# Moving four small stages of a hybrid layer's dense part, and three weight loads past a loop

## The chip, the cores and the metric

The kernel runs on one core of a Trainium2 chip. The metric is device time in microseconds (us), of the whole program. TensorE (PE in the rows) does the matrix products; VectorE (DVE), ScalarE (ACT) and GpSimd (POOL) do the elementwise work; SyncE (SP) issues the weight transfers.

## The reference

One layer for 256 tokens of width 1024, in float32, and a last norm:

```python
u = rmsnorm(h, norm1_w)
rx, rg, qkv, z, a_in, b_in, ga, gb = split_columns(u @ w_in, IN_WIDTHS)
rx = causal_dwconv(rx, rnn_conv_w) + rnn_conv_b
h_rnn = rglru(rx, wa, ba, wx, bx, lam)            # tanh/exp/sqrt, then a scan over the tokens
y_a = (jax.nn.gelu(rg) * h_rnn) @ w_branch_a
q, k, v = jnp.split(jax.nn.silu(causal_dwconv(qkv, dn_conv_w)), 3, axis=-1)
q = l2norm(q); k = l2norm(k)                      # 8 heads of 128
g = -exp(dn_a_log) * softplus(a_in + dn_dt_bias); beta = sigmoid(b_in)
o = gated_delta_rule(q, k, v, g, beta)            # chunks of 64, a triangular inverse for each
y_b = (rmsnorm(o, dn_norm_w) * silu(z)) @ w_branch_b
h = h + (sigmoid(ga) * y_a + sigmoid(gb) * y_b) @ w_out
h = h + memory_cross_attention(rmsnorm(h, norm2_w), rmsnorm(mem, mem_norm_w), w_cq, w_ckv, w_co)
h = h + hierarchical_moe(rmsnorm(h, norm3_w), ...)   # 64 experts, 2 for each token
return rmsnorm(h, norm_f_w)
```

## The kernel before

**The dense part** lasts from 0 to 536 us. Its unit of work is one piece of a weight matrix. `load_w` has SP load 1 MB into one of two buffers `raw`; for each half ACT casts it (L169) to a high part, and the remainder is formed at L170, by DVE for the first half and by GpSimd for the second. Both parts stand in `whl`, whose four buffers hold two units. Then TensorE does 48 matmuls of 128x128 by 128x256 (L178, L179, L180: high by high, high by low, low by high). Units follow one another in the order of the code: 4 for the memory's keys (`wkv`), 5 x units (the recurrence's input), 5 g units (its gelu gate), 4 value units (the memory's values), z unit 0, 12 k, q and v units (`qkv_unit`, units 0 to 3 are k), then `wa` on the recurrence's output, the z and gate units that are left, and the later projections.

Between the units stand smaller stages that other engines share:
- `memory_norm` squares the memory (ACT, L212), adds up over columns (DVE, L214), sums over partitions by small matmuls (L349, L220), takes an inverse root in DVE steps (L121 to L125) and scales the keys on GpSimd (L353).
- `recurrence(h)`, once for each half of the blocks: ten matmuls (L385), tanh and exp on ACT, long DVE operations over 128x1280, a scan (L403), a product (L404), and the split for `wa` (L154 on ACT, L155 on DVE).
- `decay` makes the decay factors of the delta rule from small products (L292 to L303); `smalls` makes constants of the recurrence.
- `squares` transposes the 16 pieces of k by matmuls against the identity (L496) and squares them on ACT with a sum (L500).
- The inverses of the delta rule's triangles are a long chain on DVE (to L610) and then products on TensorE (L630 on). `meanwhile(n)` writes n of the eleven `fill` units (z units 1 to 3, gate units 0 to 7) ahead of those products; the others are used in the chunk loop and behind it, up to the split of the delta rule's output (L762, L155), which the next dense unit (`w_branch_b`) reads.

A scheduler sets the order of instructions on each engine, from the order of the code, with priority for what a unit's `load_w` does and for the conversion behind a q, k or v unit.

**The expert part** streams 192 weight matrices of 2 MB through a ring of 10 buffers (4 `ra`, 6 `rb`; L1101, L1106 and L1109 in `load_next`). Ahead of it stands `overflow()`, a loop on the chip (L1235, L1236) whose body runs only when an expert has too many tokens. The six `rb` buffers lie where the dense part had its data. A load that has to wait for its buffer holds up what is behind it in SP's queue.

Of the kernel before, what the change touches and what calls it, by code (L numbers as in the profile page):

```python
# [41 lines left out]
def hybrid_kernel(ctx: ExitStack, tc: tile.TileContext, A, out, dbg=None, until=99):  # L42
# [204 lines left out]
    for h in range(2):  # L247
        q = slice(4 * h, 4 * h + 4)
# [33 lines left out]
    def decay():  # L282

        softplus(ga[:, 1], ga[:, 0], ga[:, 2], ga[:, 3], ga[:, 4])
        SC.activation(ga[:, 5], bcast(P("alog"), 2), AF.Exp)
        V.scalar_tensor_tensor(ga[:, 0], ga[:, 1], -1.0, ga[:, 5], op0=OP.mult, op1=OP.mult)
        gm = small("gm", [2, 2, 8])
        for cc in range(2):
            V.tensor_scalar_mul(gm[:, :, cc], ga[:, 0], C("half", cc, 1))
        pg = bank("sm")  # L290
        g16, X0, X1 = [t.rearrange("p t h -> p (t h)") for t in (ga[:, 0], X[:, 0], X[:, 1])]
        T.matmul(pg[:, 0:16], C("tri"), g16, start=True, stop=True)  # L292
        T.matmul(pg[:, 16:32], C("same"), g16, start=True, stop=True)
        T.matmul(pg[:, 32:64], ones, gm.rearrange("p t c h -> p (t c h)"), start=True, stop=True)
        V.tensor_copy(X0, pg[:, 0:16])
        V.tensor_sub(X1, pg[:, 16:32], X0)
        SC.activation(EGL.rearrange("p t c h -> p (t c h)"), pg[:, 32:64], AF.Exp)
        pm = bank("sm")
        pmv = pm[:, :48].rearrange("p (q t a c) -> p q t a c", q=3, t=2, a=4)
        for par in range(2):  # L300
            for tt in range(2):
                for cc in range(2):
                    T.matmul(pmv[HALF[par], :, tt, :, cc], ident[:, cc * 64:cc * 64 + 64], X[:, :, tt, par::2],  # L303
                             start=True, stop=True)
        V.tensor_copy(TM[:, :3], pm[:, :48].rearrange("p (q n) -> p q n", q=3))
        SC.activation(TM[:, 3:5], TM[:, 0:2], AF.Exp)
        V.tensor_scalar_mul(TM[:, 5], TM[:, 3], -0.25)
# [28 lines left out]
    def smalls():  # L336

        V.tensor_scalar_mul(ch[:, 0], P("lam"), -1.0)
        softplus(ch[:, 1], ch[:, 0], ch[:, 2], ch[:, 3], ch[:, 4])
        V.tensor_scalar_mul(ch[:, 0], ch[:, 1], -4.0)  # L340
        V.tensor_scalar_mul(ch[:, 1], ch[:, 1], 2.0)
        V.tensor_scalar_mul(hb[:, 0], P("ba"), 0.5)
        V.tensor_scalar_mul(hb[:, 1], P("bx"), 0.5)
# [12 lines left out]
    def x_unit(un_):  # L356
        w = load_w(A["win"][un_])
        p = bank()
        for m in range(2):
            dense(p[:, m * 256:m * 256 + 256], w, m, u1)  # L360
        for m in range(2):
            r = un_ * 2 + m
            conv(xc[r // HB][:, r % HB], p[:, m * 256:m * 256 + 256], P("rcw", 4 * r, 4), P("rcb", r))

    def g_unit(un_):
        w = load_w(A["win"][5 + un_])
        p = bank()
        for m in range(2):
            dense(p[:, m * 256:m * 256 + 256], w, m, u1)
        sq = t2k("gsq")  # L370
        SC.activation(sq, p, AF.Square, scale=math.sqrt(0.044715))
        V.scalar_tensor_tensor(sq, sq, 1.0, p, op0=OP.add, op1=OP.mult)
        SC.activation(sq, sq, AF.Tanh, scale=math.sqrt(2.0 / math.pi))
        for m in range(2):
            r = un_ * 2 + m
            V.scalar_tensor_tensor(gg[r // HB][:, r % HB], two(sq)[:, m], 1.0, two(p)[:, m],
                                   op0=OP.add, op1=OP.mult)

    def recurrence(h):
        tr, ti = five("tr"), five("ti")  # L380
        for b in range(HB):
            r = h * HB + b
            p = bank("gd")
            for s in range(2):
                T.matmul(p[:, s * 256:s * 256 + 256], wg[h][:, s, b], xc[h][:, b], start=True, stop=True)  # L385
                SC.activation((tr, ti)[s][:, b], p[:, s * 256:s * 256 + 256], AF.Tanh,
                              bias=hb[:, s, r:r + 1], scale=0.5)

        a = five("lra")
        for b in range(HB):  # L390
            r = h * HB + b
            SC.activation(a[:, b], tr[:, b], AF.Exp, bias=ch[:, 0, r:r + 1], scale=ch[:, 0, r:r + 1])
            SC.activation(tr[:, b], tr[:, b], AF.Tanh, bias=ch[:, 1, r:r + 1], scale=ch[:, 1, r:r + 1])
        V.scalar_tensor_tensor(tr, a, 1.0, tr, op0=OP.add, op1=OP.mult)
        V.tensor_scalar(a, tr, -1.0, 1.0, op0=OP.mult, op1=OP.add)
        V.scalar_tensor_tensor(tr, tr, -2.0, tr, op0=OP.add, op1=OP.mult)

        SC.activation(tr, tr, AF.Sqrt, scale=-1.0 / 16)
        V.scalar_tensor_tensor(ti, ti, 1.0, xc[h], op0=OP.add, op1=OP.mult)
        V.tensor_mul(ti, ti, tr)  # L400
        V.memset(a[:, :, 0:1], 0.0)
        flat = lambda t: t.rearrange("p b t -> p (b t)")
        V.tensor_tensor_scan(flat(tr), flat(a), flat(ti), 0.0, OP.mult, OP.add)  # L403
        V.tensor_mul(ti, tr, gg[h])  # L404
        dump(f"gh{h}", ti)
        hi, lo = five("ghh", FR), five("ghl", FR)
        split(hi, lo, ti)
        gh.append((hi, lo))
# [16 lines left out]

    for un_ in range(5):
        x_unit(un_)
        if un_ == 0:
            memory_norm()
    smalls()  # L430
    for un_ in range(5):
        g_unit(un_)
    for h in range(2):
        recurrence(h)
    decay()
    for un_ in range(4):
        value_unit(un_)
    if until <= 1:
# [4 lines left out]
    def z_unit(un_):  # L443
        w = load_w(A["win"][22 + un_])
        p = bank()
        for m in range(2):
            dense(p[:, m * 256:m * 256 + 256], w, m, u1)
        th = t2k("zth")
        SC.activation(th, p, AF.Tanh, scale=0.5)
        for m in range(2):  # L450
            V.scalar_tensor_tensor(zf[:, un_, :, m], two(th)[:, m].rearrange("p (c t) -> p c t", c=4), 1.0,
                                   two(p)[:, m].rearrange("p (c t) -> p c t", c=4), op0=OP.add, op1=OP.mult)
# [21 lines left out]
    def qkv_unit(un_):  # L474
        w = load_w(A["win"][10 + un_])
        p = bank()
        for m in range(2):
            dense(p[:, m * 256:m * 256 + 256], w, m, u1)
        with tc.high_priority():
            tmp, th = two(t2k("cvt")), two(t2k("cth"))  # L480
            for m in range(2):
                conv(tmp[:, m], p[:, m * 256:m * 256 + 256], P("qcw", (un_ * 2 + m) * 4, 4))
            SC.activation(th, tmp, AF.Tanh, scale=0.5)
            dst = (kf, qf, vf)[un_ // 4]
            for m in range(2):
                V.scalar_tensor_tensor(dst[:, un_ % 4, :, m], th[:, m].rearrange("p (c t) -> p c t", c=4), 1.0,
                                       tmp[:, m].rearrange("p (c t) -> p c t", c=4), op0=OP.add, op1=OP.mult)


    NK = small("nk", [8, 16])  # L490

    def squares(f, dst):
        for q in range(4):
            p = bank("gd")
            for i, (tt, hp, c) in enumerate(units[q * 4:q * 4 + 4]):
                T.transpose(p[:, i * 128:i * 128 + 128], f[:, hp, c].rearrange("p b t -> p (b t)"), ident)  # L496
            sq = t2k("sqk", tag="tg")
            for i in range(4):
                o = slice(i * 128, i * 128 + 128)
                SC.activation(sq[:, o], p[:, o], AF.Square, accum_out=dst[:, q * 4 + i:q * 4 + i + 1])  # L500

    def key_sums():
        squares(kf, NK[:, 0])

        V.tensor_scalar(NK[:, 0], NK[:, 0], 0.25, EPS, op0=OP.mult, op1=OP.add)
        rsqrt(NK[:, 2], NK[:, 0], NK[:, 3])
        V.tensor_mul(NK[:, 3], NK[:, 2], NK[:, 2])
        V.scalar_tensor_tensor(NK[:, 5], TM[:, 2], 0.5, NK[:, 3], op0=OP.mult, op1=OP.mult)
        V.tensor_scalar_mul(NK[:, 6], NK[:, 5], 0.25)
        V.scalar_tensor_tensor(NK[:, 4], NK[:, 0], 0.5, NK[:, 2], op0=OP.mult, op1=OP.mult)  # L510
# [13 lines left out]
    for un_ in range(12):  # L524
        if un_ == 1:
            z_unit(0)
        qkv_unit(un_)
        if un_ == 7:
            key_sums()
        if un_ == 9:  # L530
            query_sums()
# [85 lines left out]
            un_ = next(fill)  # L617
            z_unit(4 + un_) if un_ < 0 else gate_unit(un_)

    meanwhile(4)  # L620


    flat8 = lambda t: t.rearrange("p n i -> p (n i)")
# [552 lines left out]
                T.matmul(into[tt][h], ct[:n, tt * 128:tt * 128 + 128], Y[:n, h * 512:h * 512 + 512],  # L1176
                         start=False, stop=False, skip_group_check=True)

    for k in range(NA + NB + 1):
        if k == NA:  # L1180
            nc.sync.dma_start(half, by_halves[:, :2048])
        load_next()
# [89 lines left out]
            combine(lambda tt: opw[:, tt], Y, SLOTS)  # L1272

    overflow()
    for e in range(NE - 3):
        expert(e)

# [159 lines left out]
```

## Time and profile before

| what | us |
|---|---|
| time, median of 3 runs | 1497.77 |
| lowest, highest run | 1497.13, 1500.68 |
| profiled execution, own time | 1499.66 |
| profiled execution, span | 1497.9 |
| TensorE busy | 1109.8 |
| VectorE busy | 539.3 |
| ScalarE busy | 349.4 |
| GpSimd busy | 199.9 |

Busy times are of the profiled execution, and every start time below counts from the start of its span. Its own time is 1.8 us more than the span, for what lies around it.

### The profile page before, as it was taken

How to read it: one execution, taken by the hardware profiler on the slowest of the kernel's cores; microseconds unless marked ns; L12 is line 12 of the kernel's file. 1: busy time of each engine (PE TensorE's matmuls, PEld its weight loads, DVE VectorE, ACT ScalarE, POOL GpSimd, SP SyncE). 2: the span in 40 equal slices, each digit the busy share in tenths (PEclk: the TensorE clock that was granted, in tenths of full speed). 3: DMA queues.
4: the chain of work that ended last, by engine and by line, in shares of the span. 5: the costliest groups of instructions: out<-in, count | busy, mean ns of one | idle time of the engine just before them, and what ended most of it. 6: DMA issues, size and time to landing. Idle time of an engine off the chain costs nothing.

```text
span 1497.9 us, 33194 instructions
## 1 busy us (share of the span) xinstructions
PE 1109.8 (74%) x14941; PEld 929.0 (62%) x14941; DVE 539.3 (36%) x1217; ACT 349.4 (23%) x741; POOL 199.9 (13%) x107
## 2 busy tenths in 40 slices
PE   6998999979999957876565675756656756666575
PEld 6997999979889945654444553545544545445453
DVE  7966786675757332221111211111202111111122
ACT  5356664417435510100000000000000000000011
POOL 2443332621136200000000000000000000000000
PEclk9999998989999978998898887887979889789897
DMA  7343352521268367999999999999999999999994
GB/s 254 138 170 130 123 170 92 191 85 58 84 243 325 116 273 327 426 425 425 426 426 427 425 427 424 425 426 427 425 426 425 426 426 427 425 425 427 426 424 177
DMA packets 42002, 477.40 MB, mean 319 GB/s; under 512 B 4481, under 2 KB 7169, under 8 KB 9857
## 3 DMA queue, kind: packets, MB, share of 16 engines
q1 hardware_dynamic: 40560, 472.56, 76.9%
q8 instruction: 119, 1.95, 0.5%
q10 hardware_dynamic: 1296, 2.68, 0.5%
q14 instruction: 27, 0.21, 0.0%
HBM read 474.17 MB, written 1.05 MB: 317 GB/s over the span
## 4 chain that ended last, share of the span: by engine, by line
DMA 56%; PE 5%; DVE 0%; issue 0%; ACT 0%; DVEq 0%; SPq 0%; ACTq 0%
DMA rb<-wed 13%; DMA rb<-weu 11%; DMA rb<-weg 11%; DMA ra<-weu 8%; DMA ra<-weg 8%; DMA ra<-wed 5%; PE gd L1140 2%; PE gd L1160 1%; PE mm L1176 1%; PE gd L1131 1%; PE mm L1208 0%; ACT fsq L1329 0%; DVE goh L1002 0%; PE gd L1313 0%; PE mm L1322 0%
## 5 line engine op out<-in xcount | busy, mean ns | idle before, releaser
L1140 PE MATMUL gd<-rb,xy 128*32 128x128 f32 x4864 | 182.0, 314 | 112.7 <-DMA rb<-weu 56.8
L1140 PEld LDWEIGHTS gd<-rb,xy 128*32 128x32 f32 x4864 | 160.1, 127 | 140.1 <-DMA rb<-weu 65.0
L170 POOL TENSOR_TENSOR whl<-raw,whl 128x1024 fp32r<-128x1024 f32 (+1 forms) x66 | 161.5, 2448 | 328.5 <-ACT whl L169 324.9
L1149 DVE SCALAR_TENSOR_TENSOR hid<-hid,gd 128x128 f32<-128x128 f32 x64 | 18.4, 288 | 440.7 <-ACT hid L1148 440.7
L1140 PE MATMUL gd<-ra,xy 128*32 128x128 f32 x3168 | 120.3, 317 | 72.4 <-DMA ra<-weg 35.2
L180 PE MATMUL mm<-u1h,whl 128*128 128x256 f32 x544 | 159.0, 292 | 6.9 <-DVE whl L170 6.4
L1140 PEld LDWEIGHTS gd<-ra,xy 128*32 128x32 f32 x3168 | 106.3, 128 | 88.6 <-DMA ra<-weu 40.1
L179 PE MATMUL mm<-u1l,whl 128*128 128x256 f32 x544 | 159.9, 294 | 0.0
L178 PE MATMUL mm<-u1h,whl 128*128 128x256 f32 x544 | 159.4, 293 | 0.0
L169 ACT CAST whl<-raw 128x1024 fp32r<-128x1024 f32 (+1 forms) x132 | 131.1, 1007 | 118.5 <-PE mm L180 87.9
L1148 ACT ACTIVATE hid<-gd 128x128 f32<-128x128 f32 x64 | 17.7, 277 | 532.0 <-PE gd L1140 532.0
L1160 PE MATMUL gd<-rb,hid 128*32 128x256 f32 x1216 | 94.5, 463 | 62.9 <-DMA rb<-wed 44.2
L1165 DVE COPY xy<-gd 32x256 f32<-32x256 f32 x126 | 52.6, 418 | 236.0 <-PE gd L1160 209.4
L1165 ACT COPY xy<-gd 32x256 f32<-32x256 f32 x126 | 45.8, 364 | 314.8 <-DVE xy L1165 314.8
L180 PEld LDWEIGHTS mm<-u1h,whl 128*128 128x128 f32 x544 | 107.9, 198 | 8.3 <-DVE whl L170 7.0
L179 PEld LDWEIGHTS mm<-u1l,whl 128*128 128x128 f32 x544 | 108.1, 199 | 2.1 <-issue 1.7
L1160 PEld LDWEIGHTS gd<-rb,hid 128*32 128x32 f32 x1216 | 47.5, 128 | 99.1 <-issue 65.1
L178 PEld LDWEIGHTS mm<-u1h,whl 128*128 128x128 f32 x544 | 108.0, 198 | 1.1 <-issue 0.7
L1009 POOL TENSOR_TENSOR gpw<-goh,ew 128x512 f32<-128x512 f32 x8 | 8.4, 1046 | 747.2 <-PE sm L1171 680.3
L170 DVE TENSOR_TENSOR whl<-raw,whl 128x1024 fp32r<-128x1024 f32 (+1 forms) x66 | 82.2, 1246 | 55.3 <-ACT whl L169 54.9
L1160 PE MATMUL gd<-ra,hid 128*32 128x256 f32 x800 | 62.1, 462 | 38.7 <-DMA ra<-wed 19.6
L1131 PEld LDWEIGHTS gd<-goh,hm 128*128 128x128 f32 x512 | 61.5, 194 | 15.8 <-issue 15.8
(420 smaller groups left out, 1782.2 us busy)
## 6 DMA issues: line engine op xcount, KB each, us to landing
rb<-weu SPq DMA_DIRECT2D x38, 2048.0 KB, 39.8
rb<-wed SPq DMA_DIRECT2D x38, 2048.0 KB, 39.8
rb<-weg SPq DMA_DIRECT2D x38, 2048.0 KB, 39.8
ra<-weg SPq DMA_DIRECT2D x26, 2048.0 KB, 39.9
ra<-weu SPq DMA_DIRECT2D x25, 2048.0 KB, 39.8
ra<-wed SPq DMA_DIRECT2D x25, 2048.0 KB, 39.8
raw<-win SPq DMA_DIRECT2D x34, 1024.0 KB, 4.9
raw<-wkv SPq DMA_DIRECT2D x7, 1024.0 KB, 4.9
```

The lines of the kernel that those rows point to most:

```text
L169: (hi[j].copy if hi[j] is SC else hi[j].tensor_copy)(w[:, 0], r)
L170: lo[j].tensor_sub(w[:, 1], r, w[:, 0].bitcast(FT))
L178: T.matmul(p, w(0, i, ms), u(0, i), start=(i == 0), stop=False)
L179: T.matmul(p, w(0, i, ms), u(1, i), start=False, stop=False)
L180: T.matmul(p, w(1, i, ms), u(0, i), start=False, stop=(i == k - 1))
L1131: T.matmul(o, hm[:, tt, c * 128:c * 128 + 128], g[:, tt], start=(tt == 0), stop=(tt == 1))
L1140: m = T.matmul(p[32 * j:32 * j + 32, o:o + 128], x[:, c], w(c)[:, j * 128:j * 128 + 128], start=(c == 0), stop=(c == 7), tile_position=(0, ...
L1148: SC.activation(tg, p[:, :128], AF.Tanh, scale=0.5)
L1149: V.scalar_tensor_tensor(th, tg, 1.0, p[:, :128], op0=OP.add, op1=OP.mult)
L1160: T.matmul(p[32 * q:32 * q + 32, :256], ht[:, 32 * j:32 * j + 32], w(j)[:, o:o + 256], start=(j == 0), stop=(j == 3), tile_position=(0, 32 ...
L1165: (SC.copy if q % 2 else V.tensor_copy)(Y[r:r + 32, q * 256:q * 256 + 256], p[32 * q:32 * q + 32, :256])
L1176: T.matmul(into[tt][h], ct[:n, tt * 128:tt * 128 + 128], Y[:n, h * 512:h * 512 + 512], start=False, stop=False, skip_group_check=True)
```

## The change

The order of the code changes in five places. `memory_norm` goes from behind x unit 0 to behind g unit 0, and `smalls` from ahead of the g units to behind g unit 2. `recurrence(1)` goes from ahead of the value units to ahead of qkv unit 2, and `decay` from there to ahead of qkv unit 4. `squares` of the keys is done in two parts: its first half behind qkv unit 6, its second in `key_sums`, where all of it stood. `meanwhile` writes six units ahead of the inverse's products and not four. Of the loads ahead of `overflow()` three are written behind it.

```diff
     for un_ in range(5):
         x_unit(un_)
+    for un_ in range(5):
+        g_unit(un_)
         if un_ == 0:
             memory_norm()
-    smalls()
-    for un_ in range(5):
-        g_unit(un_)
-    for h in range(2):
-        recurrence(h)
-    decay()
+        if un_ == 2:
+            smalls()
+    recurrence(0)
     for un_ in range(4):
         value_unit(un_)
...
-    def squares(f, dst):
-        for q in range(4):
+    def squares(f, dst, qs):
+        for q in qs:
...
     def key_sums():
-        squares(kf, NK[:, 0])
+        squares(kf, NK[:, 0], (2, 3))
...
     for un_ in range(12):
         if un_ == 1:
             z_unit(0)
+        if un_ == 2:
+            recurrence(1)
+        if un_ == 4:
+            decay()
         qkv_unit(un_)
+        if un_ == 6:
+            squares(kf, NK[:, 0], (0, 1))
         if un_ == 7:
             key_sums()
...
-    meanwhile(4)
+    meanwhile(6)
...
-    for k in range(NA + NB + 1):
+
+    HELD = 3
+    for k in range(NA + NB + 1 - HELD):
         if k == NA:
             nc.sync.dma_start(half, by_halves[:, :2048])
         load_next()
...
     overflow()
+    for _ in range(HELD):
+        load_next()
     for e in range(NE - 3):
         expert(e)
```

What the scheduler makes of it is shown at three places. The first is VectorE's order around the memory's norm. Before, its sum (L214) stands between steps of the first norm's inverse root (`ny`, L123 to L125), ahead of the products with the input (L244):

```order
L125 SCALAR_TENSOR_TENSOR ny<-ny 128x256
L214 TENSOR_REDUCE nx<-memsq 128x256
L123 TENSOR_TENSOR ny<-ny 128x256
L170 TENSOR_TENSOR whl<-raw,whl 128x1024
L124 SCALAR_TENSOR_TENSOR ny<-ny,nx 128x256
L125 SCALAR_TENSOR_TENSOR ny<-ny 128x256
L244 SCALAR_TENSOR_TENSOR xn<-xx,vecs,ny 128x256 x7
```

In the changed kernel it stands in the g units, behind a gelu unit's last operations (L376), and the first step on what TensorE made of it (L350, L222) follows one L170 later:

```order
L372 SCALAR_TENSOR_TENSOR gsq<-gsq,mm 128x512
L376 SCALAR_TENSOR_TENSOR gg<-gsq,mm 128x256 x2
L214 TENSOR_REDUCE nx<-memsq 128x256
L170 TENSOR_TENSOR whl<-raw,whl 128x1024
L350 TENSOR_SCALAR rsm<-sm 128x2
L222 TENSOR_SCALAR nx<-gd 128x256
L121 TENSOR_SCALAR rsm<-rsm 128x2
L372 SCALAR_TENSOR_TENSOR gsq<-gsq,mm 128x512
```

The sum moved behind all convolutions of the x units. On TensorE the small matmuls on it (L349, L220) stood at the start of the x units; they now stand behind the 14th matmul of g unit 2, the 350th that reads `u1`.

The second place is ScalarE's order where the first half of the recurrence ends (its split L154) and the second half's tanh (L386) began. Before:

```order
L423 ACTIVATE vm<-mm,rsm 128x256 x2
L169 CAST whl<-raw 128x1024 x2
L154 CAST ghh<-ti 128x1280
L423 ACTIVATE vm<-mm,rsm 128x256
L386 ACT_TABLE_LOAD
L386 ACTIVATE tr<-gd,hbias 128x256 x2
L169 CAST whl<-raw 128x1024
L386 ACTIVATE ti<-gd,hbias 128x256 x2
```

After, two casts of weights have passed the split, and the rows behind it go on with value and k units:

```order
L169 CAST whl<-raw 128x1024 x2
L423 ACTIVATE vm<-mm,rsm 128x256 x2
L154 CAST ghh<-ti 128x1280
L169 CAST whl<-raw 128x1024 x2
L423 ACTIVATE vm<-mm,rsm 128x256 x2
L169 CAST whl<-raw 128x1024
L312 ACTIVATE cvt<-mm,vecs 128x256
```

The tanh of the second half moved behind the first k unit and z unit 0. On VectorE the second half's scan stands, before and after, ahead of the last k units' conversions (L316, and the product that was L486 and is L485). In the changed kernel:

```order
L403 SCALAR_TENSOR_TENSOR tr<-lra,ti 128x1280
L316 SCALAR_TENSOR_TENSOR cvt<-mm,vecs,cvt 128x254
L404 TENSOR_TENSOR ti<-tr,gg 128x1280
L170 TENSOR_TENSOR whl<-raw,whl 128x1024
L316 SCALAR_TENSOR_TENSOR cvt<-mm,vecs,cvt 128x253
L305 COPY tm<-sm 128x48
L155 TENSOR_TENSOR ghl<-ti,ghh 128x1280
L316 SCALAR_TENSOR_TENSOR cvt<-mm,vecs,cvt 128x255
L485 SCALAR_TENSOR_TENSOR kf<-cth,cvt 128x4x64
```

TensorE's first eight transposes of the keys (L496, now L495) stand behind q unit 6, 48 dense matmuls ahead of the other eight; before, twelve stood together behind q unit 7, and four a little later.

The third place is VectorE's order behind the chain of the inverses, whose end is L610 (now L615). Before, one gate unit's product (L467) stands ahead of the operations on TensorE's first products (L639):

```order
L608 STREAM_TRANSPOSE sta<-sta 128x512
L170 TENSOR_TENSOR whl<-raw,whl 128x1024
L610 TENSOR_SCALAR stt<-sta,early_consts 128x16x32 x2
L467 SCALAR_TENSOR_TENSOR ya<-ath,ya 128x512
L634 STREAM_TRANSPOSE stt<-stt 128x512 x2
L639 TENSOR_TENSOR yb<-gd,early_consts 64x8x64 x4
```

After, two more L170 and one more gate product stand there:

```order
L613 STREAM_TRANSPOSE sta<-sta 128x512
L170 TENSOR_TENSOR whl<-raw,whl 128x1024
L615 TENSOR_SCALAR stt<-sta,early_consts 128x16x32 x2
L466 SCALAR_TENSOR_TENSOR ya<-ath,ya 128x512
L639 STREAM_TRANSPOSE stt<-stt 128x512 x2
L170 TENSOR_TENSOR whl<-raw,whl 128x1024
L466 SCALAR_TENSOR_TENSOR ya<-ath,ya 128x512
L170 TENSOR_TENSOR whl<-raw,whl 128x1024
L644 TENSOR_TENSOR yb<-gd,early_consts 64x8x64
```

On TensorE 220 dense matmuls, before 140, stand between the last matmul of the triangles and the inverse's first product; in exchange 72, before 171, are left between the last matmul of the chunk loop (L714) and the first of `w_branch_b`. SP's queue holds six `rb` loads ahead of the loop before, and four after; two stand behind it now. (The third held load waited for an `ra` buffer and stood behind the loop in both.)

## Rows read from the trace of the kernel before

**Rows 1.** The page's second part: GB/s in 40 equal slices of the span.
```profile
GB/s 254 138 170 130 123 170 92 191 85 58 84 243 325 116 273 327 426 425 425 426 426 427 425 427 424 425 426 427 425 426 425 426 426 427 425 425 427 426 424 177
```
**Rows 2.** The chain that ended last, one piece: start, length, what.
```profile
633.40 37.90 DMA rb<-weu
```
**Rows 3.** Waits of TensorE, 0 to 540 us: total us, times, longest.
```profile
PE mm L180 <- DVE whl L170: 8.3, 5, 3.9
PE gd L630 <- DVE stt L610: 7.6, 1, 7.6
PE gd L385 <- ACT tr L386: 6.5, 1, 6.5
PE gd L496 <- ACT sqk L500: 2.5, 1, 2.5
```
**Rows 4.** Busy us by stretch: PE, PEld, DVE, ACT, POOL; granted clock, DMA share, GB/s.
```profile
77.00:82.00 5.00, 5.00 (x26) 5.00 (x25) 4.19 (x9) 2.91 (x4) 1.25 (x1) 0.50 0.58 210
158.00:182.00 24.00, 24.00 (x202) 24.00 (x202) 22.32 (x20) 17.02 (x25) 10.77 (x5) 1.00 0.44 150
187.00:196.00 9.00, 8.75 (x60) 8.54 (x59) 7.96 (x14) 6.92 (x9) 2.23 (x1) 0.81 0.34 118
323.00:330.00 7.00, 7.00 (x34) 7.00 (x34) 2.94 (x6) 0.00 (x0) 0.00 (x0) 0.50 0.28 115
564.00:576.00 12.00, 5.56 (x132) 5.13 (x132) 0.30 (x1) 0.28 (x1) 0.00 (x0) 0.60 0.38 139
```
**Rows 5.** Timeline, memory's norm and g units: start, length, instruction, [idle before <- releaser].
```profile
24.68 2.00 ACT L212 ACTIVATE memsq<-memx 128x1024 f32<-128x1024 f32 x2
30.31 3.93 DVE L214 TENSOR_REDUCE nx<-memsq 128x256 f32<-128x2048 f32 x1
68.21 4.81 DVE L289 TENSOR_SCALAR gm<-ga,early_consts 128x16 f32<-128x16 f32 x2
68.37 4.62 POOL L353 TENSOR_TENSOR kt<-kt,ny 128x2048 f32<-128x2048 f32 x1 [2.82 <-DVE ny L125]
76.43 0.58 PE L180 MATMUL mm<-u1h,whl 128*128 128x256 f32 x1 [3.88 <-DVE whl L170]
92.80 0.63 ACT L373 ACTIVATE gsq<-gsq 128x512 f32<-128x512 f32 x1 [0.75 <-DVE gsq L372]
```
**Rows 6.** Timeline from the recurrence's first half to the last k product.
```profile
145.46 1.26 ACT L154 CAST ghh<-ti 128x1280 fp32r<-128x1280 f32 x1 [6.38 <-DVE ti L404]
148.39 0.84 ACT L386 ACTIVATE tr<-gd,hbias 128x256 f32<-128x256 f32 x2
186.81 0.39 PE L180 MATMUL mm<-u1h,whl 128*128 128x256 f32 x1 [1.94 <-DVE whl L170]
189.59 0.41 DVE L486 SCALAR_TENSOR_TENSOR kf<-cth,cvt 128x256 f32<-128x256 f32 x1
205.82 0.97 DVE L486 SCALAR_TENSOR_TENSOR kf<-cth,cvt 128x256 f32<-128x256 f32 x2 [0.76 <-ACT cth L483]
```
**Rows 7.** Timeline at the inverses.
```profile
319.57 1.18 DVE L170 TENSOR_TENSOR whl<-raw,whl 128x1024 fp32r<-128x1024 f32 x1
322.02 1.30 PE L630 MATMUL gd<-stt,ab 128*128 128x64 f32 x5 [7.58 <-DVE stt L610]
```
**Rows 8.** Timeline behind the chunk loop: its last matmuls, the output's last split.
```profile
393.97 0.87 PE L714 MATMUL gd<-sm,qf 128*64 128x128 f32 x10
410.97 0.69 DVE L155 TENSOR_TENSOR ol<-ynat,oh 128x512 fp32r<-128x512 f32 x1 [0.69 <-ACT oh L154]
```
**Rows 9.** Timelines of SP and PE, and the `rb` loads' landing, 535 to 580 us.
```profile
539.41 0.44 SPq L1106 DMA_DIRECT2D rb<-weg  x1
570.44 4.75 PE L1140 MATMUL gd<-ra,xe 128*32 128x128 f32 x112 [20.41 <-SPq L1236]
573.95 0.34 SPq L1101 DMA_DIRECT2D ra<-weu  x1
DMA to landing us min/median/max: 8.6/19.9/30.0
```

## The prediction

> **What bounds the kernel now.** I read the transfer rate by slices first. From slice 17 to the last but one it stands at 424 to 427 GB/s [rows 1]: the reader is to see a stream of weights without a hole, to the end. The chain agrees: from 633.40 on its pieces are transfers [rows 2]. So the time is the moment at which this stream gets going, plus a rest that the change doesn't touch. The stream needs the six `rb` buffers, which the dense part holds to about 536 us, so whatever shortens the dense part moves the end by the same amount; so does a shorter hole in the stream at the loop.
>
> The dense part is bound by TensorE. At the full clock 202 matmuls take 24.00 us [rows 4], 0.119 each, so a unit of 48 takes 5.7. What can be won are TensorE's waits [rows 3] and the slower clock behind them: after the 3.88 us wait at 76.43 [rows 5] the granted clock is 0.50, the lower level of 1.2 GHz, and 26 matmuls take 5.00 us and not 3.1 [rows 4], 1.9 more. I take this 1.9 as the price that a wait of some microseconds has beside its length.
>
> **1. The memory's norm leaves the x units.** There VectorE is full, and GpSimd's product L353 (4.62) begins beside VectorE's L289, two operations of 128x16 that take 4.81 [rows 5]. The weights' remainder for the next unit came late behind both, and TensorE waited 3.88. Without the norm that wait goes, and its 1.9: −5.8. The rest of the norm's work only moves, and the g units have room on VectorE for it.
>
> A new wait comes. TensorE's order puts L349 62 matmuls behind the end of g unit 0, which is 7.4 us. What it needs is ScalarE's squares (2.00), VectorE's sum (3.93) [rows 5], and ahead of both the gelu unit's own conversion, three or four steps like L373's 0.63 and the 0.75 that it waited: some 2 us by estimate. That is 8 against 7.4; one cast ahead in ScalarE's queue adds 1. I take a wait of 1, without a fall of the clock: **−5**. Bounds: no wait, −6; a wait of 3 with the clock, −1.
>
> L353 now stands where GpSimd makes remainders for the g units. The row shows one VectorE operation held for as long as L353 runs, 4.81 beside 4.62. The Trainium skill ("SBUF — State Buffer", Who interferes with whom) says why and speaks against the move: VectorE and GpSimd share a port pair as an exclusive lock, and the one that comes second is blocked for the whole instruction. By that rule all of VectorE's shared reads stand still for 4.6 us wherever L353 is put, and if TensorE is at the end of its buffers there, 4.6 come back and the term is −0.4; the trace agrees as to the blocking. I keep −5: GpSimd's remainder takes 2.4 of a unit's 5.7 and two units are buffered, so one hold of 4.6 is made good within two units.
>
> **2. The recurrence's second half, `decay`, and the squares.** Before, ScalarE's queue holds the split L154 ahead of L386; it sat idle 6.38 for VectorE's L404 [rows 6], and TensorE, whose ten L385 need L386 to free banks, waited 6.5 [rows 3]. In the new order value and k units follow, whose casts stand ahead of L154 or need nothing of it. The L385 and `decay`'s small matmuls are only moved. Gone: 6.5 and 1.9 of clock. Later in the chain TensorE waited 1.94 at 186.81 for a remainder queued behind the second half's operations [rows 6], and at 0.81 of the clock 60 matmuls took 9.00 and not 7.1 [rows 4]; the transposes waited 2.5 for the squares [rows 3], which halves with a unit between them avoid. In all 6.5 + 1.9 + 1.9 + 1.9 + 2.5 = 14.7 at stake.
>
> What is late next: the eight transposes behind q unit 6 need all of k's unit 3, and the last k product stands on VectorE behind L403, L404, a remainder and L155. Behind the transposes TensorE's whole queue waits. From L386's start to the first k product behind L155 the trace has 189.59 + 0.41 − 148.39 = 41.6 us [rows 6]. TensorE has, from L385 to the transposes, five units (28.6), the L385 themselves (about 5 by estimate) and `decay` (1.5, by estimate): 35.1. It waits 6.5 and loses 1.9 of clock: 8.4. If the remainder's wait of 1.94 comes again ahead of it, it is taken from this 6.5. Net 8.4 − 14.7 = **−6**. Bounds: if the interval shrinks to 35 with VectorE freed of the value units' neighbours, −14, of which I allow −9, as some wait for remainders will stay; if it is that of k unit 3 before, 205.82 + 0.97 − 148.39 = 58.4 [rows 6], the wait is 23.3 and the net +10.5. There TensorE made unit 3 later, so I lean to the short one.
>
> **3. Six units at the inverses.** TensorE waited 7.58, to 322.02 [rows 7], and ran at 0.50 behind it: 34 matmuls in 7.00 us from 323 on [rows 4]. 96 more dense matmuls, 11.4 us, now stand ahead of the first product (80 of them directly ahead). From 314.44 they end at 325.9; gate unit 2 needs its remainder, done at 319.57 + 1.18 = 320.75 [rows 7], against 320.2, half a microsecond. So the products begin at 326.4, 4.4 later, with 11.4 of work done: −7.0. They depend on one another through VectorE, so I give the better clock only −1.
>
> The price lies at the other end. Between the last L714 (ends 394.84) and the output's last split (ends 411.66) lie 16.8 us [rows 8], which 171 dense matmuls covered; 72 are left, 8.6, and with the sixteen transposes there some 10.5 by estimate. If the chain stays 16.8 long, TensorE is dry for 6.3; if the chain was so long only because other units' work was in its queues, for none. VectorE and ScalarE did remainders, casts and conversions in between, so I take 2. Net −7 − 1 + 2 = **−6**; bounds −9 and −1.
>
> `smalls` stays where it was in VectorE's order: nothing.
>
> **4. Loads behind the loop.** The last of six loads is issued at 539.41 and lands 30.0 later, at 569.4; TensorE, held by the loop's entry, goes on at 570.44 [rows 9]. The next load waits for TensorE to free a buffer, 573.95. From 564 to 576 the share of DMA is 0.38 [rows 4]: 7.4 us of hole. With two loads (2.1 MB at 426 GB/s [rows 1], 4.9 us each) moved behind, the entry opens 9.8 us earlier, near 559.6; SP issues them some 1.5 us later (TensorE went on 1.0 after the landing), and a transfer needs some 3 us until it flows (the shortest landing of 8.6 [rows 9] less 4.9). Hole 4.7, gain **−2.7**. TensorE starts near 560.6, frees its first buffer 3.5 us on, and the two loads last longer than that, so no second hole. Bounds: 0, if the entry waits for something else than landings, and −4.5, if only 2.9 stay.
>
> **Sum:** −5 − 6 − 6 − 2.7 = −19.7. The profiled execution's own 1499.66 would be 1480.0; the median of runs is 1.9 below that execution, 1497.77, so 1478.
>
> **The rivals**
> - *New waits eat more of it.* L349 waits 3, L353's hold comes back, or the fill runs out by 6.3: each costs 2 to 5 more than taken. Two of them leave a gain of 5 to 13: 1485 to 1493. For it: VectorE is late with remainders five times before [rows 3]. Against it: two units are buffered, and the g units have room. 0.25.
> - *The keys come late (the slower side).* The interval of 58.4 gives +10.5 in part 2 against −13.7 in the others: −3.2, 1494.5, no change that can be told. Slower by over 0.3% needs k unit 3 some 66 us behind L386, 31 behind TensorE's arrival (8 more than the 58.4). For it: the second half's long operations stand ahead in VectorE's queue, and `decay`'s small ones now among them. Against it: 41.6 in the trace. No change 0.06, slower 0.04.
> - *More is won.* The keys are there in time and the fill suffices: −6 − 9 − 9 − 4 = −28, down to 1468 or a little below. 0.10.
> - *The loads do nothing*, because the loop's entry isn't bound by landings: 1480.5. This and its opposite lie within the forecast.
>
> **How the numbers follow.** The forecast (a gain of 14 to 27, 1471 to 1484) has 0.55. About 4.5 us, 0.3%, is what a measurement tells from no change. Range: the forecast's and most of the gain lost to new waits, and most of the gain of the better case: 1468 to 1491. Faster 0.55 + 0.25 + 0.10 = 0.90, same 0.06, slower 0.04.
>
> **What would show it.** Right: the end of the dense part some 17 us earlier (six loads at 536 become four at 519); no wait on L386 or at L630's successor over 1 us; a wait of 5 to 7 at the transposes of the keys, and of about 1 at L349; a hole of 3 to 5 us in the stream behind the loop. Wrong: TensorE waiting 15 us or more at the transposes, a dry TensorE ahead of `w_branch_b` over 4 us, remainders late in the g units beside L353, or a stream that is not shorter by what the dense part lost, which would mean that something else than the `rb` buffers starts it.

## The result and the profile after

The changed kernel takes 1478.3 us (median of four runs, 1475.58 to 1483.62), the kernel before, run beside it, 1498.24: ratio 0.9871, interval 0.9855 to 0.9887, 19.9 us faster. The profiled execution is the slowest of the four: own time 1483.62, span 1481.9. A second profile of the same kernel (span 1475.7) is used beside it, as the two differ in a telling way.

TensorE's waits of the first profile, 0 to 540 us (total, times, longest), to be read against [rows 3]:

```profile
PE mm L180 <- DVE whl L170: 9.5, 6, 4.5
...
PE gd L763 <- DVE otm L749: 1.9, 1, 1.9
...
PE sm L303 <- ACT egl L297: 1.5, 1, 1.5
PE gd L495 <- DVE kf L485: 1.5, 1, 1.5
PE sm L349 <- DVE nx L214: 1.4, 1, 1.4
...
PE gd L385 <- ACT ti L386: 0.7, 1, 0.7
```

The 7.6 at the inverse's product is gone, the 6.5 at L385 is 0.7, the 2.5 at the squares has become 1.5 at the keys (3.0 in the second profile). Waits for weights' remainders (L170) have not gone: 9.5 against 8.3, and the longest is now 4.5, at 312.73.

SP's timeline of the first profile around the loop:

```profile
523.88 0.33 SPq L1111 DMA_DIRECT2D rb<-weu  x1
...
525.25 1.23 SPq L1111 DMA_DIRECT2D rb<-weu  x1
549.58 0.34 SPq L1114 DMA_DIRECT2D rb<-wed  x1
...
552.55 0.33 SPq L1106 DMA_DIRECT2D ra<-weu  x1
```

The four `rb` loads' way to landing, and two stretches behind it (columns as in [rows 4]):

```profile
DMA to landing us min/median/max: 8.4/15.2/22.3
```

```profile
544.00:548.00 4.00, 0.00 (x0) 0.00 (x0) 0.00 (x0) 0.00 (x0) 0.00 (x0) 0.50 0.32 135
548.00:552.00 4.00, 3.15 (x60) 2.92 (x64) 0.00 (x0) 0.00 (x0) 0.00 (x0) 0.50 0.41 102
```

The last of the four lands at 525.25 + 22.3 = 547.5, the first held load is issued 2.0 later; the DMA shares leave a hole of 2.7 + 2.4 = 5.1 us, where it was 7.4 [rows 4].

Five marks on the timelines split the time: TensorE's first L385 (end of the gelu units), its first matmul of the query sums (L518, L519 before), its first product of the inverses, the first `rb` load, and the span's end.

| kernel | L385 | query sums | inverse | rb load | end | rb load to end |
|---|---|---|---|---|---|---|
| before | 113.29 | 245.13 | 322.02 | 536.07 | 1497.9 | 961.8 |
| after, first profile | 110.89 | 234.97 | 320.99 | 523.88 | 1481.9 | 958.0 |
| after, second profile | 107.15 | 232.61 | 315.51 | 517.74 | 1475.7 | 958.0 |

Part 1 is the change of the first mark, part 2 that of the stretch to the second, part 3 that of the next two stretches together (work moved from the later one to the earlier), part 4 that of the last:

| part | forecast | first profile | second profile |
|---|---|---|---|
| 1, norm | −5 | −2.4 | −6.1 |
| 2, recurrence, squares | −6 | −7.8 | −6.4 |
| 3, six units | −6 | −2.0 | −5.8 |
| 4, loads | −2.7 | −3.8 | −3.8 |
| sum | −19.7 | −16.0 | −22.1 |

### The profile page after: what moved, and what is told of

Read it like the earlier page. It is cut to its first block, busy times and chain, and to the rows that moved or that the text cites. A ratio compares the mean times of both kernels' runs of the same rounds, so it can differ in the third digit from the quotient of the medians.

```text
span 1481.9 us, 33189 instructions
## 1 busy us (share of the span) xinstructions
PE 1113.4 (75%) x14941; PEld 929.9 (63%) x14941; DVE 532.7 (36%) x1217; ACT 349.1 (24%) x741; POOL 202.7 (14%) x107
## 4 chain that ended last, share of the span: by engine, by line
DMA 59%; PE 3%; DVE 0%; issue 0%; ACT 0%; DVEq 0%; SPq 0%; ACTq 0%
DMA rb<-wed 13%; DMA rb<-weu 11%; DMA rb<-weg 11%; DMA ra<-weu 8%; DMA ra<-weg 8%; DMA ra<-wed 7%; PE gd L1145 1%; PE gd L1165 1%; PE mm L1215 0%; PE mm L1181 0%; PE gd L1136 0%; ACT fsq L1338 0%; PE gd L1322 0%; PE mm L1331 0%; DVEq L1442 0%
## 5 line engine op out<-in xcount | busy, mean ns | idle before, releaser
L1145 PE MATMUL gd<-rb,xy 128*32 128x128 f32 x4864 | 186.5, 318 | 112.8 <-DMA rb<-weu 55.9
L1145 PEld LDWEIGHTS gd<-rb,xy 128*32 128x32 f32 x4864 | 163.9, 128 | 140.6 <-DMA rb<-weu 64.1
L170 POOL TENSOR_TENSOR whl<-raw,whl 128x1024 fp32r<-128x1024 f32 (+1 forms) x66 | 163.4, 2476 | 313.0 <-ACT whl L169 312.9
L1154 DVE SCALAR_TENSOR_TENSOR hid<-hid,gd 128x128 f32<-128x128 f32 x64 | 18.4, 287 | 442.4 <-ACT hid L1153 442.4
L170 DVE TENSOR_TENSOR whl<-raw,whl 128x1024 fp32r<-128x1024 f32 (+1 forms) x66 | 92.3, 1398 | 58.7 <-ACT whl L169 58.5
```

What stands on the lines that cost most here:

```text
L170: lo[j].tensor_sub(w[:, 1], r, w[:, 0].bitcast(FT))
L1145: m = T.matmul(p[32 * j:32 * j + 32, o:o + 128], x[:, c], w(c)[:, j * 128:j * 128 + 128], start=(c == 0), stop=(c == 7), tile_position=(0, ...
L1154: V.scalar_tensor_tensor(th, tg, 1.0, p[:, :128], op0=OP.add, op1=OP.mult)
```

## The experiments

**The parts undone one by one**, and the changed kernel once more.

```diff
# norm back
     for un_ in range(5):
         x_unit(un_)
+        if un_ == 0:
+            memory_norm()
     for un_ in range(5):
         g_unit(un_)
-        if un_ == 0:
-            memory_norm()
# recurrence back
     recurrence(0)
+    recurrence(1)
+    decay()
...
-        if un_ == 2:
-            recurrence(1)
-        if un_ == 4:
-            decay()
...
-        if un_ == 6:
-            squares(kf, NK[:, 0], (0, 1))
# four units
-    meanwhile(6)
+    meanwhile(4)
# no load held
-    HELD = 3
+    HELD = 0
```

(With the recurrence back, all four quarters of the squares are in `key_sums` again.)

> The changed kernel once more, for a second profile. Its first profiled execution took 1483.62, the slowest of four (1475.58 to 1483.62). Theory A: the spread comes from the inverses, where gate unit 2's remainder on VectorE took 3.33 us instead of 1.23 beside GpSimd's, TensorE waited 4.49 for it and then ran 45 matmuls at half the clock (2.7 us more); an execution near 1476 to 1478 shows that wait shorter by 2 or more, or without the slow stretch. Rival B: that wait is the same (4 to 5) in every execution and the spread lies in the granted clock elsewhere, so the stretch from the triangles to the inverse's first product is as long as before, within 1 us, whatever the time.

> The changed kernel with the memory's norm behind x unit 0 again, all else as changed. Theory (the forecast's part 1): a wait of some 4 us for a weight's remainder comes back in the x units and the half clock behind it, the wait on the norm's sum in the g units (1.4) goes: 3 to 5 us slower than the changed kernel, 1481 to 1483. Rival: the lock of VectorE by GpSimd's product costs the same wherever it lies; within 1.5 us of the changed kernel, 1477 to 1480.

> The changed kernel with the recurrence's second half, the decay and the squares where they stood before. Theory (part 2, with the traces' size): the wait of 6.5 on the tanh behind the first half's split comes back, with its slow clock and the 2.5 at the squares: 6 to 10 us slower than the changed kernel, 1484 to 1488. Rival: what is won there is given back at the inverses, whose chain on VectorE is the longer one; less than 4 slower, below 1482.

> The changed kernel with four units ahead of the inverse's products and not six. Theory of the forecast (part 3): the wait of 7.6 comes back there, less what the end of the fill gives: 6 us slower than the changed kernel, 1484. Rival, from the first trace after: the six units only moved the wait from the products to gate unit 2's remainder (4.5 and a slow stretch), and the end was 2 us dry; within 2 us of the changed kernel, 1476 to 1480.

> The changed kernel with no load held back behind the loop. Theory (part 4): the loop's entry waits for every landing, the hole in the stream grows from some 5 back to 7.4 us, and TensorE starts on the experts 10 us later: 2 to 4 us slower than the changed kernel, 1480 to 1482. Rival: the loads hide it, because the stream has work queued either way; within 1 us of the changed kernel (1477.8).

| kernel | median us | ratio to before, interval | over the changed kernel's 1477.8 |
|---|---|---|---|
| changed, again | 1477.77 (1474.38 to 1478.44) | 0.9867, 0.9849 to 0.9885 | |
| norm back | 1482.93 | 0.9902, 0.9885 to 0.9918 | 5.2 |
| recurrence back | 1486.23 | 0.9915, 0.9889 to 0.9942 | 8.5 |
| four units | 1482.93 | 0.9911, 0.9894 to 0.9927 | 5.2 |
| no load held | 1481.66 | 0.9892, 0.9875 to 0.9908 | 3.9 |

By the medians every part is worth something, 0.2 to 2.5 us off its forecast, and each rival missed. The intervals say less: those with the recurrence back and with four units lie above the changed kernel's, that with the norm back begins where it ends (0.9885), and that with no load held overlaps it. So the profiles have to decide, and in them what the forecast had named came back. The first L385 begins at 114.29 with the norm back, and at 105.6 to 110.9 in the ten profiles with the norm and the recurrence where the changed kernel has them. The stretch to the query sums is 131.6 with the recurrence back, 131.8 before, and 124.1 and 125.5 in the changed kernel's two. With no load held, the hole behind the loop's entry (columns as in [rows 4]):

```profile
553.00:565.00 12.00, 6.31 (x142) 5.42 (x146) 1.56 (x5) 0.56 (x2) 0.00 (x0) 0.68 0.36 132
```

That is 7.7 us, as before (7.4), where the changed kernel has 5.1. The stretch from the first `rb` load to the end, 960.1 in this profile, decides nothing: it is 957.1 to 960.6 in the nine profiles with the loop and three loads held. With the norm back, on the timeline:

```profile
77.21 0.58 PE L180 MATMUL mm<-u1h,whl 128*128 128x256 f32 x1 [5.44 <-DVE whl L170]
...
69.06 4.75 DVE L289 TENSOR_SCALAR gm<-ga,early_consts 128x16 f32<-128x16 f32 x2
...
69.22 4.57 POOL L353 TENSOR_TENSOR kt<-kt,ny 128x2048 f32<-128x2048 f32 x1 [2.82 <-DVE ny L125]
```

The same pair as in [rows 5], with a longer wait behind it. With the recurrence back and with four units (two kernels, their waits):

```profile
PE gd L385 <- ACT tr L386: 6.5, 1, 6.5
PE gd L497 <- ACT sqk L501: 2.4, 1, 2.4
```

```profile
PE gd L635 <- DVE stt L615: 7.6, 1, 7.6
```

The second profile answered the first of these expectations: theory A holds, with one correction. These are the timelines of the two profiles at gate unit 2, the first one above:

```profile
309.26 2.34 POOL L170 TENSOR_TENSOR whl<-raw,whl 128x1024 fp32r<-128x1024 f32 x1 [4.18 <-ACT whl L169]
...
309.35 3.33 DVE L170 TENSOR_TENSOR whl<-raw,whl 128x1024 fp32r<-128x1024 f32 x1
...
312.73 0.58 PE L180 MATMUL mm<-u1h,whl 128*128 128x256 f32 x1 [4.49 <-DVE whl L170]
```

```profile
307.16 1.18 DVE L170 TENSOR_TENSOR whl<-raw,whl 128x1024 fp32r<-128x1024 f32 x1
...
307.27 3.32 POOL L170 TENSOR_TENSOR whl<-raw,whl 128x1024 fp32r<-128x1024 f32 x1 [4.38 <-ACT whl L169]
...
308.40 0.39 PE L180 MATMUL mm<-u1h,whl 128*128 128x256 f32 x1 [2.33 <-DVE whl L170]
```

The stretch behind the wait in the first profile:

```profile
314.00:321.00 7.00, 7.00 (x43) 7.00 (x43) 3.53 (x6) 1.05 (x1) 0.00 (x0) 0.66 0.79 293
```

Both engines make one half's remainder of the same unit, and they begin within 0.11 us of each other. Where GpSimd is 0.09 ahead, its own takes 2.34 and VectorE's 3.33; where VectorE is 0.11 ahead, its own takes 1.18 and GpSimd's 3.32. TensorE needs VectorE's first. That is the difference of a wait of 4.49 with 43 matmuls in the 7 us behind it, and a wait of 2.33. Six more profiles have six units with these remainders divided in the same way: in five of these VectorE's comes second, takes 3.3 to 3.4, and TensorE waits 4.5; in the sixth it takes 1.18, and the wait is 2.3. From the query sums to the first product the two profiles differ by 3.1 us; the correction is that the rest of the 6.1 between their spans lies ahead of the query sums (2.4) and behind the first product (0.7).

**Where the wait at gate unit 2 can be put.** The first kernel has VectorE make both remainders of that unit; the second has five units ahead of the products.

```diff
# gate 2 on VectorE
-        w = load_w(A["win"][26 + un_])
+        w = load_w(A["win"][26 + un_], lo=(V, V) if un_ == 2 else (V, G))
# five units
-    meanwhile(6)
+    meanwhile(5)
```

> The changed kernel with both remainders of gate unit 2 made by VectorE, none by GpSimd; on VectorE the second one stands between the two halves of the chain's last step. Theory: in the changed kernel the two remainders of this unit begin within 0.1 us of each other, and whichever comes second is held: VectorE's takes 3.33 in one profile (TensorE waits 4.5, slow clock behind it), 1.18 in the other (it waits 2.3). Without GpSimd's the better case holds in every execution: VectorE's first remainder 1.2, the wait near 2.3, runs within 4 us of each other and none over 1480, median 1474 to 1477. Rival: the spread is the clock's own, and the second remainder only lengthens the chain by 1.2; median 1478 to 1480 with a spread of 4 to 8 as before.

> The changed kernel with five units ahead of the inverse's products. Theory: the unit that is waited for (gate unit 2, 2.3 to 4.5) goes into the chunk loop, where TensorE is idle for short stretches anyway, and the dry end ahead of the next weight matrix (1.9) goes; but TensorE now waits some 4 for the chain's end itself: within 2 us of the changed kernel, 1476 to 1479. Rival (the forecast's reckoning): each unit less ahead of the products costs its share of the wait, half of what four units cost (5.2): 1480 to 1481.

Both expectations fell. With gate 2 on VectorE the median of six runs is 1487.48 (0.99, 0.9859 to 0.9941): two at 1473 and 1474, four at 1487 to 1489. At its own place the edit did more than was expected: the profiled execution has the first remainder in 1.18, no wait of TensorE's over 0.6 is left ahead of the products, and it begins the inverse's products at 312.02, 3.5 earlier than the better profile above. But then (its timeline, and a stretch behind it):

```profile
314.86 2.58 POOL L170 TENSOR_TENSOR whl<-raw,whl 128x1024 fp32r<-128x1024 f32 x1 [4.80 <-ACT whl L169]
...
315.74 2.26 DVE L466 SCALAR_TENSOR_TENSOR ya<-ath,ya 128x512 f32<-128x512 f32 x1
...
318.76 0.32 PE L635 MATMUL gd<-stt,yb 128*128 128x64 f32 x1 [1.81 <-DVE yb L644]
```

```profile
324.00:330.00 6.00, 6.00 (x30) 6.00 (x30) 1.41 (x2) 0.00 (x0) 0.00 (x0) 0.50 0.00 0
```

The next unit's remainder on GpSimd holds VectorE's gate product (2.26, elsewhere 0.67), the next operations on the products (L644) stand behind it, and TensorE waits 1.81 between two products. The granted clock falls to 0.50 and stays there from 320 to 346, past the end of the products at 342.2, though TensorE is busy all the while. The same stretch in the changed kernel's second profile:

```profile
322.00:328.00 6.00, 6.00 (x55) 6.00 (x55) 3.80 (x6) 0.00 (x0) 0.00 (x0) 1.00 0.24 98
```

55 matmuls in 6 us, not 30. From the first product to the last it is 30.2 us here and 17.9 there: a wait of 1.8 us would have cost 12, itself included, if the slow clock is its doing; the next experiment takes it away. With five units the median of seven runs is 1482.18 (1478.14 to 1497.35; 0.9929, 0.9894 to 0.9963), at or above the changed kernel, by which the rival is nearer. Its profiled execution, the fastest, waits 5.9 for the chain's end and stands at 0.50 behind it, and the dry end of 1.9, which was to go, is still there; the 1497 was not seen in a profile.

**VectorE's operations on the products first**, with gate 2 on VectorE and without:

```diff
     for lev in (16, 32):
         p = products(AB, TS)
+        with tc.high_priority():
-        for g in range(2):
-            for hf in HALF:
-                V.tensor_mul(YB[hf, GR[g], hf], p[g][hf], ...)
+            for g in range(2):
+                for hf in HALF:
+                    V.tensor_mul(YB[hf, GR[g], hf], p[g][hf], ...)
...
             if lev == 16:
+                with tc.high_priority():
-                V.tensor_copy(US[:, GR[g]], p[g])
-                V.transpose(flat8(TS[:, GR[g]]), flat8(US[:, GR[g]]))
+                    V.tensor_copy(US[:, GR[g]], p[g])
+                    V.transpose(flat8(TS[:, GR[g]]), flat8(US[:, GR[g]]))
```

> The kernel with gate unit 2's remainders on VectorE, and besides VectorE's operations on the inverse's products ahead of gate unit 2's own product. Theory: what made the kernel without it slow (1488 in four of six executions, 1473 and 1474 in two) is this: VectorE's gate product, ahead of the products' operations, took 2.26 us beside a remainder of GpSimd's, TensorE waited 1.8 in the middle of the inverse's products, and ran them at half the clock for 24 us, 12 lost. With the gate product behind them that wait goes: median 1472 to 1475, and no execution over 1480. Rival: the slow clock there comes from the thin work of the products themselves; some executions stay at 1486 to 1489.

> The changed kernel with VectorE's operations on the inverse's products ahead of gate unit 2's own product, and nothing else. Theory: in the changed kernel this wait doesn't occur, and the two remainders of gate unit 2 still begin within 0.1 us of each other: median and spread stay those of the changed kernel, 1474 to 1483 with the median near 1478. Rival: the gate product is itself in the way of the products; 2 us faster or more, median 1476 or below.

With both edits no run lies at 1487 to 1489: 1476.87 (1473.72 to 1482.27; 0.9857, 0.9834 to 0.988). In its profile no such wait is left between the products, they run at 1.00 and take 18.4. That bears out the cause of the long ones; the size expected (1472 to 1475, none over 1480) was missed, and the kernel can't be told from the changed one. Its profiled execution is the slowest of its four; its first `rb` load is at 519.94, and from there to the end it takes 960.6, 2.6 more than in the changed kernel's profiles, though nothing was edited there. Without gate 2 on VectorE the reordering takes 1481.86 (0.9892, 0.9867 to 0.9916), at or above the changed kernel, which neither theory nor rival said. Its profile has the wait of 4.5 at gate 2 again. Both profiles with the reordering lose time behind the products: from the last product to the first `rb` load 187.8 and 187.0, where the changed kernel's two take 185.0 and 184.4, and TensorE's wait of 1.9 at the dry end is 2.4.

**The loop.** Five loads held, and no loop at all (the work for experts with too many tokens is left out).

```diff
# five held
-    HELD = 3
+    HELD = 5
# no loop
-    overflow()
```

> The changed kernel with five loads behind the loop and not three, so two of 2 MB ahead of it and not four. Theory: the hole is the way from the last landing through the loop's entry to the next load's first bytes, some 5 us, however many loads lie ahead, as long as the loop's count (ready some 12 us behind the first load's issue in the changed kernel) comes before the last landing: the hole moves 10 us earlier, the time is that of the changed kernel within 1.5 us. The two loads' landing and the count then nearly coincide, so 1 to 2 us more of hole are possible. Rival: the entry's price falls with the number of loads ahead of it; 2 to 4 us faster, near 1474.

> The changed kernel without the loop: it leaves out the work for experts with too many tokens, of which these inputs have none, so only the loop's entry goes. Theory: the loop costs the hole that the stream still has behind its entry, 5.1 us by the DMA shares of the first profile after (2.7 between 544 and 548, 2.4 to 552); 4 to 6 us faster than the changed kernel, 1472 to 1474. Rival: without the loop the stream only runs ahead to the next wait for a buffer of TensorE's, and the hole comes there; within 1.5 us, 1476 to 1479.

Five held: 1477.6 (0.986, 0.9841 to 0.9879), as the theory said; the first load behind the entry is issued 15.4 us behind the first `rb` load (520.51 to 535.96) and not 25.7, 2.1 behind the landing of the second one (DMA to landing 13.0, from 520.89), and `rb` load to end is 958.6 against 958.0. What counts is the way from a landing through the entry to the next load, not how many lie ahead. No loop: 1468.42 (0.9807, 0.9787 to 0.9827), 9.4 faster and not 4 to 6. By its profile the hole is gone, and `rb` load to end is 951.9, 5.2 to 8.7 less than in the nine profiles with the loop and three loads held. The 4 us that its median gains beyond the hole's 5.1 stay open.

**The norm alone**, in the kernel before:

```diff
     for un_ in range(5):
         x_unit(un_)
-        if un_ == 0:
-            memory_norm()
     smalls()
     for un_ in range(5):
         g_unit(un_)
+        if un_ == 0:
+            memory_norm()
```

> The kernel before with the memory's norm behind g unit 0, and nothing else. Theory (the forecast's part 1): 5 us faster than the kernel before, 0.9967 of its time, 1490 to 1493, with TensorE's wait of 3.9 in the x units gone and one of 1 to 1.5 on the norm's sum. Rival: undoing the four parts one by one costs 5.2, 8.5, 5.2 and 3.9, 22.8 in all, where all four together give 19 to 20; if the parts overlap, the norm alone gives less, 1 to 3 us, 1494 to 1496, the recurrence's wait behind it growing by what TensorE comes earlier.

Twelve runs, median 1495.69, 0.9992 (0.9967 to 1.0016): no change that can be told, 1490.01 to 1508.19, four of them above 1501. The profiled one (1494.33) has what the theory says at the place: the first L385 at 109.01, 4.3 earlier, and a wait of 1.4 on the norm's sum. In this execution the rival's return of the gain at the recurrence didn't come: L386 is waited for 6.5, as before, and the query sums are 4.3 earlier too. What makes four executions 7 to 14 us longer than it is on no profile.

## Why the prediction was right, and where not

The time, 1478.3, is the forecast's 1478, and for all four parts the profiles show what the forecast named. That it fits to a microsecond is luck: the two profiles' sums are −16.0 and −22.1, and the terms of part 3 were wrong in opposite directions.

- **Part 1.** The wait of 3.88 went; the new one on the norm's sum is 1.4, taken as 1. The forecast had no fall of the clock behind it: in the first profile there is one (0.86 on the mean from 88 to 100), in the second none (1.00). How much the part gives depends on the execution. Ahead of both places, from 44 to 60, the granted clock is 0.79 in the kernel before and in the first profile, and 0.89 in the second and with the norm back. Like compared with like, it is 2.4 (the first profile, with the slow clock behind its new wait) and 7.1 (the second, against the norm back). Alone in the kernel before, the part shows in the profile and not in the median. By the Trainium skill's rule on the shared ports ("SBUF — State Buffer", Who interferes with whom) the engine that comes second is blocked for the other's whole instruction; the forecast's rival had VectorE stand still for 4.6 wherever L353 is put. In the changed kernel:

```profile
106.49 5.53 POOL L353 TENSOR_TENSOR kt<-kt,ny 128x2048 f32<-128x2048 f32 x1 [3.35 <-DVE ny L125]
```

```profile
110.77 2.33 DVE L170 TENSOR_TENSOR whl<-raw,whl 128x1024 fp32r<-128x1024 f32 x1 [1.17 <-ACT whl L169]
```

  VectorE's remainder beside L353 takes 2.33 where 1.2 is usual, its gelu operations in between are as fast as elsewhere (L372 in 0.68), and no wait of TensorE follows. The lock is real, and a place with room made it free, as reckoned.
- **Part 2.** The wait on L386 and the one at the squares went as said. The keys: from L386's start (159.29) to the last k product (198.63 + 0.41) it is 39.8 us, taken as 41.6. TensorE waited 1.45 there and not 6.5, because it came later, not because the keys came sooner: the 35.1 became 39.9 (157.73 to 197.65, behind the first six transposes). L303 of `decay` waited 1.5, unforeseen, L385 0.7, and the clock behind L303's wait was slow (0.86 on the mean from 185 to 197). In the second profile the clock is 1.00 there, TensorE comes after 38.7, and it waits 3.0. The slower-side rival, an interval of 58.4, didn't come near.
- **Part 3.** The place was right and the reckoning of gate unit 2 was not: "gate unit 2 needs its remainder, done at 319.57 + 1.18 = 320.75 [rows 7], against 320.2, half a microsecond". The remainder stands ahead of the chain's last step (L615), as read from the order, but VectorE and GpSimd then wanted the ports at once: the wait is 2.3 or 4.5. The Trainium skill ("SBUF — State Buffer", Who interferes with whom) adds to its rule that issue order and not the shape of an operation decides who is blocked; the two profiles, 0.1 us either way, agree. The rule was weighed at L353, and the place where it decided was the one where it wasn't looked for. So the term of −7.0 was −0.4 in the first profile and −3.5 in the second: from the query sums the products begin 9.1 and 6.0 later than before, with 80 more dense matmuls done, 9.5 us at 0.119. Against it the better clock gave some 3.9 and not 1: the products take 17.9 us from first to last and not 22.9, of which nine dense matmuls fewer among them are 1.1. That the second profile's −5.8 is so near to −6 is luck. The dry end, taken as 2, is 1.9 (L763).
- **Part 4.** The entry does wait for the last landing, and the hole is 5.1 us, taken as 4.7. The forecast's "some 3 us" until a transfer flows is 8.6 less 4.9, which is 3.7; with that and its 1.5 the hole comes to 5.2. So 2.3 of it went, taken as 2.7. The marks' 3.8 is more than the hole gave, but the stretch from which it is read scatters by 3.5 from profile to profile, so the rest can't be put down to the loads.

## What to carry to other kernels

A wait that is taken off TensorE comes back at the next operation that is late; reckon that one by its interval from the same start, and count the slow clock behind every wait, since a wait of 1.8 us at the wrong place cost 12. A mark on one profile has the clock of that execution in it: compare it at the same granted clock, or over several profiles. Where VectorE and GpSimd share one unit's work, look for the places at which both begin at once: there a tenth of a microsecond decides who is held, and the kernel's time scatters from run to run. A loop's entry on the DMA-issuing queue drains the transfers ahead of it, so loads that can be issued behind it shorten the hole: from 7.4 to 5.1 with three held. With five held the time is the same.

## What the runs showed that was not expected

The same code in the same order scatters in its first 110 us: TensorE's first L385 begins at 105.6 to 110.9 in the ten profiles of kernels that leave the norm and what stands ahead of it as in the changed kernel, and the recurrence too. They stand in the order of the granted clock. From 44 to 104, in the first profile (L385 at 110.89), the second (107.15) and that with five units (105.59), columns as in [rows 4]:

```profile
44.00:104.00 60.00, 58.59 (x450) 58.23 (x450) 45.79 (x93) 27.49 (x38) 23.94 (x10) 0.91 0.46 159
```

```profile
44.00:104.00 60.00, 58.61 (x475) 58.35 (x475) 49.12 (x101) 29.81 (x40) 24.51 (x10) 0.97 0.51 176
```

```profile
44.00:104.00 60.00, 58.60 (x487) 58.35 (x487) 49.73 (x103) 30.10 (x40) 26.87 (x10) 1.00 0.51 176
```

In all ten the mean is 0.91 where L385 begins at 110.9 and 110.7, 0.94 at 109.35 and 108.45, 0.97 at 107.05 to 107.15, and 1.00 at 106.45 to 105.59. Why it falls in one execution and not in another stays open.

And the slow clock can hold through 26 us in which TensorE is busy without a break, with 128x64 products and few dense matmuls between them (30 in 6 us, at 0.50), while the same work begun at 1.00 stays there (55 in 6 us). It needn't hold so long: in the kernel before, the same products began at 0.50 behind the wait of 7.6, and from 331 to 345 the clock is 0.99.
